# Weight-block sums of the seven-product duals: accumulating DMAs on GpSimd's queue in place of VectorE and GpSimd adds

## The chip, the cores and the metric

The kernel runs on one core of one Trainium2 chip. A core has TensorE (PE in the profile, with its weight loads as PEld), VectorE (DVE), ScalarE (ACT), GpSimd (POOL) and SyncE (SP), and 16 DMA engines that all queues share. The metric is the device time of one execution in microseconds, the median of several runs; lower is better.

## What is computed

One layer of a streaming encoder on a sequence of 1024 tokens with 1024 channels, all in fp32: a mixing sub-layer and a feed-forward sub-layer, each behind an RMS norm that is scaled and shifted by a condition vector.

```python
h = rms_norm(x, norm_mix_g) * (1.0 + sc1) + sh1
proj = h @ w_in                                   # 1024 -> 7 x 1024 columns
y_a = (b_s * causal_dwconv(c_s * v_s, conv_short_w)) @ w_short_out
u = causal_dwconv(v_c * sigmoid(gl_c), conv_conf_w) + conv_conf_b    # width 31
y_b = silu(layer_norm(u, conf_ln_g, conf_ln_b)) @ w_conf_out
x = x + g1 * ((g_a * y_a + g_b * y_b) @ w_o)
h2 = rms_norm(x, norm_ffn_g) * (1.0 + sc2) + sh2
a, bgate = split(h2 @ w_ffn_in)                   # 1024 -> 2 x 2816
x = x + g2 * ((silu(a) * bgate) @ w_ffn_out)
return rms_norm(x, final_norm_g)
```

## The kernel before

**Numbers as two parts.** Every fp32 operand of a matrix product is cut into a high and a low part that TensorE takes at its fast rate. For a weight block `raw` in SBUF, `split_w` (line 195) makes `wh`, a rounded copy written by ScalarE (line 201), and `wl = raw - wh`, written by VectorE or GpSimd (line 202). `mm3` (from line 269) then issues three matmuls per block: wh with the high and the low part of the activations (lines 273 and 274), and wl with the high part (line 276).

**Seven products for eight.** The input projection, the FFN input and all but the last part of the FFN output are done in duals: two by two blocks of the weights (11, 12, 21, 22) and of the activations, multiplied by a Winograd-like scheme with seven block products. The products come in the order `PRODUCTS = "1265734"` (line 91). Products 1, 2 and 4 use the weight blocks 11, 12 and 22 as loaded. The other four use sums of blocks:

- s1 = 21 + 22, for product 5 (line 222),
- 21 = 21 + 11, in place, for product 7 (line 223),
- 11 = 11 + s1, in place, for product 6 (line 224),
- 12 = 12 + 11, in place, after 11 has become the sum, for product 3 (line 226).

The first three are made when the weights of product 6 are prepared, the fourth when those of product 3 are. There are 12 duals in the input projection (`eng=nc.gpsimd`, so sums and `wl` are GpSimd's), 11 in the FFN input and 6 in the FFN output (both with VectorE). Blocks are 128x1024 fp32 (512 KB), in the FFN output 128x768 (384 KB). The first two duals of the FFN input are `early`: their blocks 21, 22 and 11 are loaded again when product 6 is prepared, s1 takes the place of 22, and 12 and 22 are loaded again for products 3 and 4. In all other duals the four blocks are loaded once, when product 1 is prepared, and s1 is written to a buffer of its own, `raw_tile(n)`.

**Buffers.** `raw_tile` (line 182) takes the buffers in turn from pools that hold five raw tiles together, and six from the second part of the FFN input on. `wh` and `wl` have three buffers each. `next_w` (line 241) prepares the weights of a product two products ahead. Weights are loaded by SP's queue (line 189).

**Other work on the queues.** In the input projection VectorE also computes the width-31 convolution (line 604), and SP stores and later loads the gated short-conv operands (`q_store`). In the FFN input the hidden values are combined, split on ScalarE and VectorE into three stage buffers, and stored to DRAM by DMAs on GpSimd's queue (`hid<-stage`, line 841). The FFN output reads them back by DMAs on GpSimd's queue (`th<-hid` and `tl<-hid`, line 867), six loads of 256 KB for each product, into a pool of 58 tiles. The order of the instructions on each engine's queue, DMA issues included, isn't the order of the code: a planner puts them in order by the times at which it computes them to be ready, with the order of the code as priority, and the chip then keeps to that order. A DMA that has to wait for a semaphore holds its issuing engine's queue.

Of the kernel before, what the change touches and what calls it, by code (L numbers as in the profile page):

```python
# [37 lines left out]
ALU = mybir.AluOpType  # L38
# [67 lines left out]
def block_kernel(ctx: ExitStack, tc: tile.TileContext, xT, c, vecs, ada, w_first, w_plain, w_duals,  # L106
                 w_short, w_conf, w_o, w_fi, w_fo, w_last, outT):
    nc = tc.nc
# [73 lines left out]
    def raw_tile(n=1024):  # L182

        raws.append(raws.pop(0))
        return raws[-1].tile([P, 1024], F32, tag="raw", name="raw")[:, :n]

    def load(src, n=1024):
        raw = raw_tile(n)
        nc.sync.dma_start(raw, src)
        return raw  # L190
# [4 lines left out]
    def split_w(raw, n, after=(), lo_engine=nc.vector):  # L195
        wh = whp.tile([P, 1024], F32R, tag="wh", name="wh")[:, :n]
        wl = wlp.tile([P, 1024], F32R, tag="wl", name="wl")[:, :n]
        with ExitStack() as order:
            for ins in after:
                order.enter_context(tc.issue_after(ins))  # L200
            nc.scalar.copy(wh, raw)  # L201
            lo_engine.tensor_tensor(wl, raw, f32(wh), ALU.subtract)  # L202
        return wh, wl

    def dual_units(mats, n, early=False, eng=nc.vector):

        a = {}

        def get(*blocks):
            for b in blocks:  # L210
                a[b] = load(mats[("11", "12", "21", "22").index(b)], n)

        def unit(m):
            if early:
                get(*{"1": ("11",), "2": ("12",), "6": ("21", "22", "11"), "3": ("12",), "4": ("22",)}.get(m, ()))
            elif m == "1":
                get("11", "12", "21", "22")
            if m in "12":
                return split_w(a["1" + m], n, (), eng)
            if m == "6":  # L220
                a["s1"] = a["22"] if early else raw_tile(n)
                eng.tensor_tensor(a["s1"], a["21"], a["22"], ALU.add)
                eng.tensor_tensor(a["21"], a["21"], a["11"], ALU.add)
                eng.tensor_tensor(a["11"], a["11"], a["s1"], ALU.add)
            elif m == "3":
                eng.tensor_tensor(a["12"], a["12"], a["11"], ALU.add)
            return split_w(a[{"6": "11", "5": "s1", "7": "21", "3": "12", "4": "22"}[m]], n, (), eng)

        return {m: (lambda m=m: unit(m)) for m in PRODUCTS}
# [695 lines left out]
    n = 2 * GROUP * P  # L925
# [164 lines left out]
```

## Time and profile before

| | us |
|---|---|
| median of 3 runs | 1544.36 (1543.83 to 1546.57) |
| profiled execution, own time | 1546.12 |
| its span, first to last instruction | 1544.4 |
| PE busy | 1472.5 |
| DVE busy | 1187.2 |
| ACT busy | 639.6 |
| POOL busy | 575.9 |

The profile is of one execution. Rows of the timeline read: start in us, duration in us, engine, line of the kernel, operation, output <- input by the program's names, shapes, count, and in brackets the idle time of the engine before it with what ended it. Rows of grouped instructions end in: busy us, mean ns of one | idle us before them, and what ended most of it. A DMA issue shows on its engine's queue for the issue alone; the rows of DMA issues give KB each and the median us from issue to landing. Matmuls are pipelined, so their rows overlap.

### The profile page before, as it was taken

The page shows a single profiled execution, that of the slowest core. Times are in us where ns is not written, and L with a number is a line of the kernel's source. Part 1 is how long each engine was busy: PE and PEld are TensorE (multiplying, and loading weights), DVE is VectorE, ACT ScalarE, POOL GpSimd, SP SyncE. Part 2 cuts the span into 40 slices and gives each one's busy share as a digit, 9 for nine tenths or more (in the row PEclk, how much of TensorE's full clock was granted, in tenths as well). Part 3 has the DMA queues.
Part 4 walks back from the last instruction along what each step waited for, and adds up shares of the span by engine and source line. Part 5 has one row for each costly group of instructions (what it writes and reads, how often), then busy time and mean ns, then how long its engine had stood idle before and what let it go on. Part 6 is the DMA issues. An engine that isn't in the chain of part 4 may idle for free.

```text
span 1544.4 us, 17865 instructions
## 1 busy us (share of the span) xinstructions
PE 1472.5 (95%) x6466; PEld 1208.6 (78%) x6466; DVE 1187.2 (77%) x1543; ACT 639.6 (41%) x896; POOL 575.9 (37%) x491
## 2 busy tenths in 40 slices
PE   5799999999999998989899989999999999999996
PEld 3588887888887887768788868888888888788885
DVE  7887899999998965656865798876767665677756
ACT  6563334333333342344334564444444443221235
POOL 1316778688768883310111101100100016445005
PEclk9999999999999999999999999999999999999998
DMA  9332214223222269455754428544444449999403
GB/s 369 143 100 75 95 55 164 68 96 109 96 82 95 92 230 386 144 184 164 243 191 166 164 82 258 191 150 150 151 150 156 156 151 348 349 308 274 125 14 110
DMA packets 88024, 256.16 MB, mean 166 GB/s; under 512 B 10112, under 2 KB 12288, under 8 KB 87936
## 3 DMA queue, kind: packets, MB, share of 16 engines
q1 hardware_dynamic: 47248, 147.01, 28.5%
q0 software_dynamic: 36944, 95.44, 19.1%
q10 hardware_dynamic: 3744, 12.58, 2.0%
q8 instruction: 50, 0.82, 0.2%
q14 instruction: 38, 0.31, 0.1%
HBM read 188.41 MB, written 66.58 MB: 165 GB/s over the span
## 4 chain that ended last, share of the span: by engine, by line
PE 47%; DVE 3%; issue 1%; ACT 0%; DVEq 0%; ACTq 0%
PE x L276 7%; PE x L273 7%; PE x L274 7%; PE z L273 4%; PE z L274 4%; PE z L276 4%; PE y L273 3%; PE y L276 2%; PE y L274 2%; PE mix L276 2%; PE mix L273 2%; PE mix L274 2%; PE yb L274 1%; PE yb L276 1%; PE yb L273 1%
## 5 line engine op out<-in xcount | busy, mean ns | idle before, releaser
L201 ACT CAST wh<-raw 128x1024 fp32r<-128x1024 f32 (+2 forms) x260 | 262.1, 1009 | 439.5 <-PE x L274 99.7
L202 POOL TENSOR_TENSOR wl<-raw,wh 128x1024 fp32r<-128x1024 f32 (+1 forms) x95 | 247.3, 2608 | 154.5 <-ACT wh L201 149.6
L202 DVE TENSOR_TENSOR wl<-raw,wh 128x1024 fp32r<-128x1024 f32 (+2 forms) x165 | 189.1, 1147 | 58.3 <-ACT wh L201 55.7
L604 DVE SCALAR_TENSOR_TENSOR c<-diff,vec,c 128x512 f32<-128x512 f32 x248 | 182.2, 749 | 3.9
L841 POOL DMA_DIRECT2D hid<-stage x71 | 37.8, 534 | 354.1 <-DVE stage L313 350.9
L273 PE MATMUL x<-th,wh 128*128 128x512 f32 x336 | 130.8, 389 | 0.0
L276 PE MATMUL x<-th,wl 128*128 128x512 f32 x336 | 130.7, 389 | 0.0
L274 PE MATMUL x<-tl,wh 128*128 128x512 f32 x336 | 130.7, 389 | 0.0
L604 DVE SCALAR_TENSOR_TENSOR c<-u,wsum,c 128x512 f32<-128x512 f32 x112 | 84.0, 750 | 2.0
L273 PE MATMUL x<-t2h,wh 128*128 128x512 f32 x184 | 73.8, 402 | 5.9 <-ACT wh L201 4.5
L276 PE MATMUL x<-t2h,wl 128*128 128x512 f32 x184 | 73.8, 402 | 4.7 <-POOL p L519 3.4
L274 PE MATMUL x<-t2l,wh 128*128 128x512 f32 x184 | 73.7, 401 | 0.1
L273 PEld LDWEIGHTS x<-th,wh 128*128 128x128 f32 x336 | 63.1, 188 | 13.2 <-issue 0.3
L274 PEld LDWEIGHTS x<-tl,wh 128*128 128x128 f32 x336 | 63.1, 188 | 13.2
L276 PEld LDWEIGHTS x<-th,wl 128*128 128x128 f32 x336 | 63.1, 188 | 13.1
L273 PE MATMUL z<-th,wh 128*128 128x512 f32 x168 | 65.4, 389 | 1.5 <-ACT wh L201 1.5
L258 DVE CUSTOM_DVE_ANT_0 raw<-raw,cs,vec 128x1024 f32<-128x1024 f32 x24 | 30.7, 1281 | 45.7 <-DMA raw<-in_ada 45.7
L276 PE MATMUL z<-th,wl 128*128 128x512 f32 x168 | 65.4, 389 | 0.0
L274 PE MATMUL z<-tl,wh 128*128 128x512 f32 x168 | 65.4, 389 | 0.0
L312 ACT CAST stage<-g 128x512 fp32r<-128x512 f32 x62 | 38.3, 620 | 56.5 <-DMA hid<-stage 29.3
L273 PE MATMUL yb<-zsh,wh 128*128 128x512 f32 x128 | 49.5, 400 | 10.4 <-ACT zsh L304 9.4
L313 DVE TENSOR_TENSOR stage<-g,stage 128x512 fp32r<-128x512 f32 x62 | 42.5, 688 | 20.0 <-ACT stage L312 20.0
(819 smaller groups left out, 4087.5 us busy)
## 6 DMA issues: line engine op xcount, KB each, us to landing
hid<-stage POOLq DMA_DIRECT2D x71, 512.0 KB, 4.3
raw<-in_w_fi SPq DMA_DIRECT2D x50, 512.0 KB, 4.3
raw<-in_w_duals SPq DMA_DIRECT2D x48, 512.0 KB, 3.5
th<-hid POOLq DMA_DIRECT2D x71, 256.0 KB, 6.1
tl<-hid POOLq DMA_DIRECT2D x71, 256.0 KB, 6.3
ada<-in_ada SPq DMA_DIRECT2D x24, 512.0 KB, 7.5
raw<-in_ada SPq DMA_DIRECT2D x24, 512.0 KB, 4.3
raw<-in_w_fo SPq DMA_DIRECT2D x24, 384.0 KB, 6.1
```

Source lines behind the costliest of these rows:

```text
L201: nc.scalar.copy(wh, raw)
L202: lo_engine.tensor_tensor(wl, raw, f32(wh), ALU.subtract)
L258: nc.vector.tensor_tensor_reduce(out=raw, in0=raw, in1=cs, scale=1.0, scalar=col(V_ADA, b), op0=ALU.mult, op1=ALU.add, accum_out=modc(b),)
L273: nc.tensor.matmul(ps, wh, xh, start=first, stop=False, skip_group_check=again)
L274: nc.tensor.matmul(ps, wh, xl, start=False, stop=False, skip_group_check=again)
L276: mm3.ins = nc.tensor.matmul(ps, wl, xh, start=False, stop=last, skip_group_check=again).ins
L312: nc.scalar.copy(hi, src)
L313: nc.vector.tensor_tensor(lo, src, f32(hi), ALU.subtract)
L604: nc.vector.scalar_tensor_tensor(out=out, in0=src[:, s : s + H], scalar=wt, in1=acc, op0=ALU.mult, op1=ALU.add)
L841: nc.gpsimd.dma_start(hid_dram[key], s)
```

## The change

The sums are no longer instructions of VectorE or GpSimd. Each is a DMA issued from GpSimd's queue that adds one SBUF tile to another (`accum_op=ALU.add`). Since an accumulating DMA adds to what its destination holds, s1 of a dual that isn't early is now made by loading block 22 a second time into the buffer of s1, and adding 21 to it.

```diff
             if m == "6":
-                a["s1"] = a["22"] if early else raw_tile(n)
-                eng.tensor_tensor(a["s1"], a["21"], a["22"], ALU.add)
-                eng.tensor_tensor(a["21"], a["21"], a["11"], ALU.add)
-                eng.tensor_tensor(a["11"], a["11"], a["s1"], ALU.add)
+                a["s1"] = a["22"] if early else load(mats[3], n)
+                nc.gpsimd.dma_start(a["s1"], a["21"], accum_op=ALU.add)
+                nc.gpsimd.dma_start(a["21"], a["11"], accum_op=ALU.add)
+                nc.gpsimd.dma_start(a["11"], a["s1"], accum_op=ALU.add)
             elif m == "3":
-                eng.tensor_tensor(a["12"], a["12"], a["11"], ALU.add)
+                nc.gpsimd.dma_start(a["12"], a["11"], accum_op=ALU.add)
             return split_w(a[{"6": "11", "5": "s1", "7": "21", "3": "12", "4": "22"}[m]], n, (), eng)
```

## The prediction

> **What bounds the kernel now.** I read the page first, then busy time by stage, then what TensorE (PE) waits for, and last the timeline of one dual of each stage. The first two lines are busy time by engine and the chain that ended last, by engine.
>
> ```profile
> PE 1472.5 (95%) x6466; PEld 1208.6 (78%) x6466; DVE 1187.2 (77%) x1543; ACT 639.6 (41%) x896; POOL 575.9 (37%) x491
> ...
> PE 47%; DVE 3%; issue 1%; ACT 0%; DVEq 0%; ACTq 0%
> ```
>
> Then busy us by stage: input projection in duals, FFN input, FFN output (columns PE, PEld, DVE, ACT, POOL, granted clock, DMA share, GB/s).
>
> ```profile
> 110.00:590.00 480.00, 475.12 (x2082) 392.24 (x2081) 421.18 (x523) 183.74 (x249) 361.91 (x164) 0.99 0.32 110
> 925.00:1315.00 390.00, 389.73 (x1709) 322.07 (x1708) 278.88 (x348) 171.92 (x249) 61.66 (x116) 0.99 0.57 186
> 1315.00:1490.00 175.00, 173.48 (x765) 143.11 (x764) 118.08 (x152) 39.87 (x51) 55.62 (x105) 1.00 0.74 231
> ```
>
> The sums exist in these three stages (and at 870 to 925, the head of the FFN), and PE is busy 99% of each: 475 of 480, 389.7 of 390, 173.5 of 175 us. VectorE and GpSimd are not the bound, so taking work off them pays only where PE waits for them. Those waits (total, times, longest):
>
> ```profile
> PE mu L632 <- DVE tot L629: 4.8, 1, 4.8
> PE x L273 <- ACT wh L201: 4.5, 1, 4.5
> ...
> PE x L276 <- POOL p L519: 3.4, 1, 3.4
> ```
>
> About 13 us is the most that can be won; the 4.5 us is the one that a sum causes directly.
>
> **What is removed.** Three sums in a row and a fourth per dual, 29 duals.
>
> ```profile
> L201 ACT CAST wh<-raw 128x1024 fp32r<-128x1024 f32 x202 | 212.0, 1051 | 319.1 <-PE z L274 61.7 <-issue 55.0 <-PE x L274 37.3
> ...
> L222 POOL TENSOR_TENSOR raw<-raw 128x1024 f32<-128x1024 f32 x12 | 29.5, 2456 | 41.5 <-DVE wl L202 39.4 <-DVE c L604 1.4
> ```
>
> In the 12 duals of the input projection four POOL adds of about 2.5 us, some 120 us of POOL; in 11 FFN-input duals four DVE adds of 1.22 us (the L222 row at 1104.17 below), 54 us; in six FFN-output duals four of 0.96 us (the row at 1386.06), 23 us. All of it lies beside PE, except at the head of the FFN.
>
> **What comes in.** 116 accumulating DMAs on POOL's queue, and 27 reloads of block 22 on SP's (12 + 9 + 6 duals that are not early). Within one dual they form a chain: s1 += 21 needs the reload landed; 21 += 11 overwrites what the first one reads, so POOL waits for its landing; 11 += s1 waits for the second. Only then can ScalarE cast 11 for product 6. Three adds that cost 3.7 us (DVE) or 7.5 us (POOL) become a reload and three complete DMA round trips. The price of an accumulating DMA from SBUF to SBUF is in no row. The nearest rows (KB, us to landing):
>
> ```profile
> hid<-stage POOLq DMA_DIRECT2D x71, 512.0 KB, 4.3
> raw<-in_w_fi SPq DMA_DIRECT2D x50, 512.0 KB, 4.3
> raw<-in_w_duals SPq DMA_DIRECT2D x48, 512.0 KB, 3.5
> th<-hid POOLq DMA_DIRECT2D x71, 256.0 KB, 6.1
> ...
> raw<-in_w_fo SPq DMA_DIRECT2D x24, 384.0 KB, 6.1
> ...
> x_dram<-x POOLq DMA_DIRECT2D x16, 256.0 KB, 3.0
> ```
>
> POOL's own stores go from 3.0 us for 256 KB to 4.3 for 512 KB: 1.3 us per 256 KB. Lower end for 512 KB: the second operand is read for nothing, 4.3 us. If it counts as 1 MB moved: 4.3 + 2.6 = 6.9. Upper end, two full transfers one after the other: 8.6. I take the middle of the first two, 5.6 us, as the nearest rows are those of POOL's stores, plus 0.4 us per link for POOL's issue and a weight op that stands in front: 6.0 us a link. For 384 KB the same steps give 3.65 and 5.6, middle 4.6, 5.0 with the 0.4.
>
> The Trainium skill, "Collectives: The Full Stack", The bandwidth ceiling, says that a reducing DMA is slowed by its second source read and not by the add; "DMA: Bandwidth & Descriptors", Anatomy of one DMA, puts a POOL-issued DMA at 2.0 us plus bytes at 436 GB/s. Together, as an estimate, 4.4 us for 1 MB read, 4.8 with the 0.4, by which the sum below would come out at no loss in two of three stages. The same fit would give 3.2 us for the hid store, which took 4.3 here, so the trace is above it.
>
> **Input projection.** One dual: the last weight split of the dual before, its first sum, and product 6's first matmul:
>
> ```profile
> 263.39 2.40 POOL L202 TENSOR_TENSOR wl<-raw,wh 128x1024 fp32r<-128x1024 f32 x1 [3.03 <-ACT wh L201]
> 265.86 2.40 POOL L222 TENSOR_TENSOR raw<-raw 128x1024 f32<-128x1024 f32 x1
> ...
> 289.44 0.39 PE L273 MATMUL x<-t2h,wh 128*128 128x512 f32 x1
> ```
>
> Five raw buffers serve five blocks, so s1 gets its buffer only when the previous dual's block 22 is split, at 265.79 (263.39 + 2.40); the sum starts 0.07 us later. After the change the reload starts there. To product 6 there are 289.44 - 265.79 = 23.65 us, less the cast 1.05 and the POOL split 2.4: 20.2. Less the reload 3.5: 16.7, or 5.6 us a link. A link of 6.0 is late by 3 x 0.4 = 1.2 us a dual; over 11 duals (the first has its data long before) 13 us. The DMA wait itself holds POOL, and behind it stand the splits wl of products 1 and 2, which PE needs 10 to 16 us before product 6: another 0.5 us a dual, 5 us. Behind the reload on SP stand the next blocks' loads and the q stores, which come later anyway: nothing. Term: **+18 us**.
>
> **FFN input.** The same with DVE splits; POOL's hid store is shown since it shares the queue:
>
> ```profile
> 1102.91 1.23 DVE L202 TENSOR_TENSOR wl<-raw,wh 128x1024 fp32r<-128x1024 f32 x1 [4.22 <-ACT wh L201]
> 1104.17 1.22 DVE L222 TENSOR_TENSOR raw<-raw 128x1024 f32<-128x1024 f32 x1
> ...
> 1119.09 0.53 POOL L841 DMA_DIRECT2D hid<-stage  x1 [24.41 <-DVE stage L313]
> ...
> 1129.06 0.39 PE L273 MATMUL x<-t2h,wh 128*128 128x512 f32 x1
> ```
>
> From 1104.14 to 1129.06 are 24.9; less cast 1.05 and split 1.23, 22.6; less the reload 4.3, 18.3: 6.1 us a link against 6.0. Term: **0**, and no reserve. POOL stands idle 24.4 us before the hid store, which covers the first two links; the third and the fourth accumulate fall among the stores. If they are ahead in the queue, the stage buffers (three) come free later and ScalarE waits with its casts; that is the cost if the cover goes.
>
> **FFN output.** Here a dual lasts 28 us, and POOL's queue carries the bursts of th and tl loads. The page's DMA line, then one dual in a gap between bursts:
>
> ```profile
> DMA  9332214223222269455754428544444449999403
> ```
>
> ```profile
> 1384.88 0.95 DVE L202 TENSOR_TENSOR wl<-raw,wh 128x768 fp32r<-128x768 f32 x1
> 1386.06 0.96 DVE L222 TENSOR_TENSOR raw<-raw 128x768 f32<-128x768 f32 x1 [0.24 <-DMA raw<-in_w_fo]
> ...
> 1404.41 0.39 PE L273 MATMUL x<-th,wh 128*128 128x512 f32 x1
> ```
>
> From 1385.83 to 1404.41 are 18.6; less the split 0.95 and a cast of 0.8 (three quarters of the 1.05 above, as 768 of 1024 columns), 16.8; less a reload of 6.1, 10.7: 3.6 us a link. A link of 5.0 is late by 3 x 1.4 = 4.2 us. In a burst (four to five slices at 9 in the DMA line) a POOL load of 256 KB lands after 6.1 where a quiet store takes 3.0, so I add 3.1 to each link: 3 x 4.5 = 13.5 us late. The th and tl tiles of a burst come free only as PE uses them up, so a stalled PE thins it; I count three duals of each sort: 3 x 4.2 + 3 x 13.5 = 53. Term: **+53 us**. Behind the waiting accumulates stand th and tl loads, for which PE waits a group later; with that much lead I cost them at nothing.
>
> **Head of the FFN.** Two early duals whose sums stand in DVE's line:
>
> ```profile
> 923.13 1.05 ACT L201 CAST wh<-raw 128x1024 fp32r<-128x1024 f32 x1 [5.28 <-DVE raw L224]
> ...
> 924.23 0.80 PE L273 MATMUL x<-t2h,wh 128*128 128x512 f32 x1 [4.54 <-ACT wh L201]
> ```
>
> Here DVE is late, not the data, and POOL is nearly free. The DMAs can run ahead while DVE makes the tokens' operands. Gain 4.5 us at most, and the splits next in DVE's line are then late; I take **-4**. The other waits in the list (mean of the conv, memset on POOL) may shrink too, -2.
>
> **Sum:** 18 + 0 + 53 - 4 - 2 = +65 us on the profiled span of 1544.4: 1609. The profiled execution took 1546.1 with what lies around its span; the runs without a profile have a median of 1544.36, so the span stands for them within 0.1 and **1609 us** is the prediction.
>
> **Rivals.**
> A, the chain is hidden and the time is the same or a little less. It decides at a link of 5.6 us in the projection, 6.1 in the FFN input and 3.6 to 4 in the FFN output. At the lower end (4.3 + 0.4 = 4.7, and 3.65 + 0.4 = 4.05 for 384 KB) the first two cost nothing, quiet output duals 1.4 each, burst ones perhaps 4: between -6 and +10 us, 1538 to 1554. For it: the 3.5 us loads and a DMA share of 0.32 and 0.57. Against: the hid row of 4.3 for one plain pass. The two pages of the Trainium skill named above lead here too. Chance 0.24: faster 0.12, same 0.07, slower 0.05.
> B, the accumulate runs at half rate or worse. At 7.5 us (7.9 a link): projection 3 x 2.3 x 11 = 76, FFN input 3 x 1.8 x 9 = 49, FFN output about 85: +210, 1750. At 8.6, 1830. For it: two reads per write, and th's 6.1 for 256 KB. Against: half the 16 engines' time is free. Chance 0.24.
> C, the planner that orders each engine's queue puts product 5, whose s1 is ready after one link, ahead of 6. That gives PE 5 us of other work and takes most of the projection's loss and part of the output's: +15 to +35, 1560 to 1580. For it: POOL's order already departs from the written one (first sum of a dual ahead of its first split). Against: it orders by planned times, and a DMA planned shorter than it is changes nothing. Chance 0.10.
>
> **Chances.** Forecast (1575 to 1680) 0.42, A 0.24, B 0.24, C 0.10. Within 0.2%, about what a measurement of this kernel can tell from no change (1541.3 to 1547.5): faster 0.12, same 0.08, slower 0.80. The forecast's own range is 1575 to 1680. The range given reaches into A, which leaves out the best of it, and into B as far as 1750: 1538 to 1750.
>
> **What would show it.** The median time to landing of the new raw<-raw rows decides: 5.6 forecast, under 4.7 rival A, over 7 rival B. In the waits of PE, x <- ACT wh at L201 should appear once per dual, short in the projection, long in the FFN output, with L201 in turn waiting for a DMA. If the matmul order at the start of a dual is 1, 2, 5, 6, it is C. The forecast is wrong if the FFN output is not the stage that loses most, or if hid stores on POOL wait for raw<-raw and pull the FFN input down.

## The result, and the profile after

The changed kernel takes 1666.69 us (median of 4 runs, 1660.23 to 1676.03), the kernel before 1544.09 us in the same session (4 runs): ratio 1.0796, 95% interval 1.0742 to 1.0849. That is 123 us slower; the forecast was 1609, 65 us slower. The profiled execution has a span of 1662.9 us.

From the page of the kernel after: busy time by engine, the clock of PE and the DMA share in 40 slices, and the chain that ended last, by engine and by line.

```profile
PE 1500.9 (90%) x6466; PEld 1215.4 (73%) x6466; DVE 1129.4 (68%) x1475; ACT 633.0 (38%) x896; POOL 542.5 (33%) x559
...
PEclk9999999999999999989999999999999996899898
DMA  9345556465555696556656697777777799979712
...
PE 9%; DMA 3%; issue 1%; DVE 1%; ACT 0%; POOL 0%; DVEq 0%; ACTq 0%; POOLq 0%
DMA raw<-raw 2%; PE x L273 1%; PE x L276 1%; PE x L274 1%; PE y L276 1%; PE y L274 1%; PE y L273 1%; PE z L274 1%; PE z L273 1%; PE z L276 1%; DMA th<-hid 0%; ACT wh L201 0%; DMA raw<-in_w_fo 0%; DVE sq L982 0%; DVE y L995 0%
```

The diff did what it says: DVE is busy 58 us less and POOL 33 us less. But PE, which does exactly the same 6466 matmuls, is busy 28 us longer (1472.5 before) and idle 90 us longer. The chain before was 47% PE. Now it is 9% PE and 3% DMA: the profile can follow only a small part of it, but the largest single line of that part is `DMA raw<-raw`, which didn't exist before.

Busy us by stage of the kernel after (PE, PEld, DVE, ACT, POOL, granted clock, DMA share, GB/s): input projection, FFN input, FFN output.

```profile
124.70:617.20 492.50, 470.66 (x2017) 382.30 (x2015) 415.82 (x515) 174.98 (x239) 260.06 (x159) 0.98 0.61 168
902.50:1357.40 454.90, 431.40 (x1852) 348.24 (x1851) 270.49 (x356) 196.97 (x290) 92.28 (x145) 0.99 0.79 222
1357.40:1600.60 243.20, 184.52 (x757) 147.54 (x756) 102.45 (x136) 37.82 (x51) 85.20 (x145) 0.87 0.84 232
```

The edges are the first matmuls of the stages. The kernel before, cut at the same matmuls:

```profile
124.90:590.40 465.50, 460.62 (x2017) 380.24 (x2016) 410.14 (x518) 178.37 (x241) 349.50 (x160) 0.99 0.33 113
877.10:1308.60 431.50, 425.13 (x1852) 348.42 (x1851) 319.59 (x403) 199.54 (x290) 58.29 (x110) 0.99 0.53 173
1308.60:1482.00 173.40, 171.88 (x758) 141.79 (x757) 120.47 (x156) 39.94 (x51) 59.54 (x113) 1.00 0.79 247
```

All three stages lost: 27.0, 23.4 and 69.8 us. Length less PE busy is PE's idle time. It grew by 17.0 us (4.9 to 21.8), 17.1 us (6.4 to 23.5) and 57.2 us (1.5 to 58.7). The rest of each loss is matmuls that took longer: 10.0, 6.3 and 12.6 us.

**The link.** Landing of the new transfers and of two neighbours (KB, us from issue to landing):

```profile
raw<-raw POOLq DMA_DIRECT2D x92, 512.0 KB, 4.6
hid<-stage POOLq DMA_DIRECT2D x71, 512.0 KB, 5.6
...
raw<-in_w_fi SPq DMA_DIRECT2D x59, 512.0 KB, 5.3
...
raw<-raw POOLq DMA_DIRECT2D x24, 384.0 KB, 4.5
```

An accumulating DMA takes 4.6 us, where the prediction took 5.6. The neighbours slowed down by 1.0 to 1.3 us (4.3 before).

**Who waits.** PE's waits (total, times, longest):

```profile
PE x L273 <- ACT wh L201: 47.4, 6, 26.8
PE x L273 <- ACT g L816: 16.7, 12, 4.0
...
PE z L273 <- ACT wh L201: 9.2, 1, 9.2
...
PE x L273 <- ACT sig L535: 4.4, 2, 4.1
PE x L276 <- POOL wl L202: 4.2, 5, 1.6
PE x L273 <- ACT p L535: 3.3, 2, 2.5
```

Two kinds. `wh L201` is the weight itself that is late. `g L816`, `sig` and `p L535` are ScalarE's copies of finished products out of PE's accumulators: PE waits there though the weights it needs next may be ready. One projection dual on three engines shows how that comes about:

```profile
319.91 0.88 POOL L222 DMA_DIRECT2D raw<-raw  x1 [4.08 <-issue]
...
324.74 0.88 POOL L223 DMA_DIRECT2D raw<-raw  x1 [1.51 <-DMA raw<-raw]
...
330.92 0.88 POOL L224 DMA_DIRECT2D raw<-raw  x1 [2.70 <-DMA raw<-raw]
...
335.53 1.04 ACT L201 CAST wh<-raw 128x1024 fp32r<-128x1024 f32 x1 [10.53 <-DMA raw<-raw]
336.48 0.58 ACT L535 COPY m<-x 128x512 f32<-128x512 f32 x1
...
337.11 0.50 PE L273 MATMUL x<-t2h,wh 128*128 128x512 f32 x1 [2.64 <-ACT m L535]
```

The links are 4.83, 6.18 and 4.61 us apart. ScalarE stands 10.53 us at the cast of product 6, which waits for the third link. The copy behind it in its queue starts only then, and PE waits 2.64 us for that copy.

**FFN output.** The first dual, then the clock before it, after it and, in the projection, right behind PE's wait of 2.95 us that ended at 225.75:

```profile
1343.39 0.33 SPq L189 DMA_DIRECT2D raw<-in_w_fo  x1
...
1367.72 0.89 POOL L222 DMA_DIRECT2D raw<-raw  x1 [0.95 <-DMA tl<-hid]
...
1376.08 0.88 POOL L223 DMA_DIRECT2D raw<-raw  x1 [1.76 <-issue]
...
1381.45 0.89 POOL L224 DMA_DIRECT2D raw<-raw  x1 [1.30 <-DMA raw<-raw]
...
1391.62 2.30 ACT L201 CAST wh<-raw 128x768 fp32r<-128x768 f32 x3 [19.63 <-DMA raw<-raw]
...
1392.50 0.79 PE L273 MATMUL x<-th,wh 128*128 128x512 f32 x1 [26.78 <-ACT wh L201]
```

```profile
1355.00:1365.50 10.50, 10.50 (x48) 8.54 (x46) 4.78 (x7) 2.84 (x5) 8.10 (x16) 1.00 1.20 353
...
1392.00:1396.50 4.50, 4.00 (x9) 2.95 (x10) 2.70 (x3) 1.92 (x3) 3.47 (x7) 0.50 1.27 398
...
226.20:229.50 3.30, 3.30 (x10) 2.53 (x9) 3.19 (x6) 3.30 (x6) 2.78 (x2) 0.50 0.00 0
```

Block 22 was asked for again at 1343.39, but the first sum is issued 24.3 us later: POOL's queue in between holds th and tl loads and hid stores. Then the three links take 23.9 us. After the 26.78 us stall the granted clock is 0.50, so the stall goes on costing.

### The profile page after: what moved, and what is told of

Read it like the earlier page. It is cut to its first block, busy times and chain, and to the rows that moved or that the text cites. A ratio compares the mean times of both kernels' runs of the same rounds, so it can differ in the third digit from the quotient of the medians.

```text
span 1662.9 us, 18058 instructions
## 1 busy us (share of the span) xinstructions
PE 1500.9 (90%) x6466; PEld 1215.4 (73%) x6466; DVE 1129.4 (68%) x1475; ACT 633.0 (38%) x896; POOL 542.5 (33%) x559
## 5 line engine op out<-in xcount | busy, mean ns | idle before, releaser
L201 ACT CAST wh<-raw 128x1024 fp32r<-128x1024 f32 (+2 forms) x260 | 260.1, 1008 | 551.9 <-DMA raw<-raw 244.7
L202 POOL TENSOR_TENSOR wl<-raw,wh 128x1024 fp32r<-128x1024 f32 (+1 forms) x95 | 243.8, 2611 | 144.4 <-ACT wh L201 141.0
L202 DVE TENSOR_TENSOR wl<-raw,wh 128x1024 fp32r<-128x1024 f32 (+2 forms) x165 | 188.6, 1148 | 124.6 <-ACT wh L201 121.9
L273 PE MATMUL x<-th,wh 128*128 128x512 f32 x336 | 136.1, 405 | 52.9 <-ACT wh L201 47.0
L276 PE MATMUL x<-th,wl 128*128 128x512 f32 x336 | 135.2, 402 | 0.5 <-POOL wl L202 0.5
L274 PE MATMUL x<-tl,wh 128*128 128x512 f32 x336 | 134.5, 400 | 0.0
L273 PEld LDWEIGHTS x<-th,wh 128*128 128x128 f32 x336 | 65.6, 195 | 70.4 <-ACT wh L201 49.1
L273 PE MATMUL x<-t2h,wh 128*128 128x512 f32 x184 | 77.9, 425 | 25.6 <-ACT g L816 15.1
L222 POOL DMA_DIRECT2D raw<-raw x29 | 25.7, 885 | 229.4 <-DMA raw<-in_w_fi 46.5
L276 PE MATMUL x<-t2h,wl 128*128 128x512 f32 x184 | 76.7, 417 | 5.4 <-POOL wl L202 3.3
L841 POOL DMA_DIRECT2D hid<-stage x71 | 41.3, 591 | 117.7 <-DVE stage L313 116.3
L276 PEld LDWEIGHTS x<-th,wl 128*128 128x128 f32 x336 | 65.2, 194 | 16.8 <-DVE wl L202 2.2
L273 PE MATMUL z<-th,wh 128*128 128x512 f32 x168 | 66.4, 395 | 9.3 <-ACT wh L201 9.2
L273 PEld LDWEIGHTS x<-t2h,wh 128*128 128x128 f32 x184 | 37.1, 202 | 40.1 <-ACT g L816 19.6
L276 PE MATMUL z<-th,wl 128*128 128x512 f32 x168 | 66.1, 393 | 0.3 <-DVE wl L202 0.3
```

The source lines that it names most:

```text
L222: nc.gpsimd.dma_start(a["s1"], a["21"], accum_op=ALU.add)
L273: nc.tensor.matmul(ps, wh, xh, start=first, stop=False, skip_group_check=again)
L274: nc.tensor.matmul(ps, wh, xl, start=False, stop=False, skip_group_check=again)
L276: mm3.ins = nc.tensor.matmul(ps, wl, xh, start=False, stop=last, skip_group_check=again).ins
L841: nc.gpsimd.dma_start(hid_dram[key], s)
```

## The experiments

Theory 1, formed from the profile after: the price isn't the transfers but that **each sum waits for the landing of the one before and every queue is in order**. ScalarE stands at product 6's cast with PE's evacuations behind it, and POOL's sums stand among other DMAs. Rival: the transfers themselves (71 MB more are moved, 327.2 for 256.2) slow everything down. A narrower rival for the FFN input: the hid stores behind the waiting sums on POOL.

Lengths of the stages in the profiled execution of each kernel, in us; before's profile has a span of 1544.4:

| kernel | projection | middle | FFN input | FFN output | tail | median | ratio to before, 95% |
|---|---|---|---|---|---|---|---|
| before | 465.5 | 286.7 | 431.5 | 173.4 | 62.5 | 1544.09 | |
| after | 492.5 | 285.3 | 454.9 | 243.2 | 62.3 | 1666.69 | 1.0742 to 1.0849 |
| traffic | 489.0 | 286.2 | 430.3 | 197.2 | 62.4 | 1593.93 | 1.0308 to 1.0362 |
| order_125 | 473.8 | 285.0 | 451.5 | 244.1 | 62.3 | 1646.82 | 1.0641 to 1.0688 |
| cast6_pool | 471.1 | 284.7 | 453.5 | 248.8 | 62.2 | 1648.23 | 1.0648 to 1.0718 |
| bufs | 472.9 | 280.6 | 437.3 | 233.0 | 62.3 | 1613.00 | 1.0404 to 1.0494 |
| bufs_125 | 468.7 | 276.8 | 436.6 | 236.9 | 62.2 | 1605.65 | 1.0372 to 1.0418 |
| hid_on_sp | 491.6 | 286.9 | 458.3 | 246.8 | 62.3 | 1670.45 | 1.0764 to 1.0878 |
| hid_sp_cast6 | 471.4 | 282.6 | 448.4 | 246.9 | 62.4 | 1641.89 | 1.0569 to 1.0703 |
| t_on_sp | 490.8 | 280.9 | 460.8 | 246.0 | 62.7 | 1670.21 | 1.0783 to 1.0862 |
| half_t | 491.7 | 284.1 | 459.0 | 206.0 | 62.1 | 1629.09 | 1.0504 to 1.0602 |
| no_chain | 461.9 | 288.3 | 442.7 | 208.1 | 62.3 | 1590.18 | 1.0294 to 1.0324 |
| m3_only | 458.7 | 284.9 | 430.7 | 189.0 | 62.8 | 1553.00 | 1.0053 to 1.0081 |
| e4_early | 465.5 | 286.1 | 432.8 | 171.4 | 62.2 | 1547.29 | 1.0015 to 1.0049 |

The FFN input again, cut at the first matmuls of its duals: us over the kernel before, whose two early duals take 88.7 us, the third dual 38.1 and the other eight 304.6.

| kernel | two early duals | third dual | other eight |
|---|---|---|---|
| after | 2.3 | 7.0 | 14.0 |
| traffic | -1.2 | 0.0 | 0.0 |
| order_125 | 16.5 | 0.0 | 3.5 |
| cast6_pool | 8.1 | 3.7 | 10.2 |
| bufs | -5.5 | 8.2 | 3.2 |
| bufs_125 | 0.7 | 1.7 | 2.8 |
| hid_on_sp | -0.1 | 11.7 | 15.3 |
| hid_sp_cast6 | 4.5 | 12.4 | 0.0 |
| t_on_sp | 2.7 | 10.0 | 16.6 |
| half_t | 5.1 | 8.8 | 13.7 |
| no_chain | 6.1 | 5.1 | 0.0 |
| m3_only | -1.5 | 0.7 | 0.0 |
| e4_early | 1.3 | 0.0 | 0.0 |

The edits of t_on_sp and half_t are meant for the next stage, and yet their three columns differ from after's by up to 3 us. Differences of that size aren't read here.

### Traffic without a chain (traffic)

The kernel before, with two plain stores of block 22 on POOL's queue at each of products 6, 5, 7 and 3. Nothing reads what they store.

```diff
+    spare = []
...
+            if m in "6573" and not early:
+                for _ in range(2):
+                    nc.gpsimd.dma_start(dram.tile([P, n], F32, name=f"spare{len(spare)}"), a["22"])
+                    spare.append(0)
             return split_w(a[{"6": "11", "5": "s1", "7": "21", "3": "12", "4": "22"}[m]], n, (), eng)
```

> The kernel before, its sums on VectorE and GpSimd as they were, plus eight plain 512 KB (384 KB) stores of block 22 to unused DRAM per dual that is not early, two each when the weights of products 6, 5, 7 and 3 are prepared: 216 stores that nothing waits for, on GpSimd's queue. They move at least as many bytes through the 16 DMA engines as the change does, without its chain of waits. Chain theory (the loss is the time from the freed buffer over reload and three round trips to product 6, passed on by the in-order queues of ScalarE and GpSimd): 1544 to 1560 us. Traffic theory (DMA share went from 0.33 to 0.61 in the projection and from 0.54 to 0.79 in the FFN input, hid stores from 4.3 to 5.6 us): 1600 us or more, with all three stages longer.

Neither number came: 1593.93. By stage it reads better. First the stages, then who waits, and one stall of the FFN output, in this kernel (its L202, L203, L223, L278 and L281 are L201, L202, L222, L273 and L276 of the others):

```profile
126.00:615.00 489.00, 468.97 (x2018) 381.48 (x2017) 424.26 (x518) 178.48 (x242) 399.35 (x250) 0.99 0.56 205
901.10:1331.40 430.30, 423.89 (x1851) 347.47 (x1850) 318.17 (x403) 197.95 (x290) 93.24 (x177) 0.99 0.75 258
1331.40:1528.60 197.20, 174.20 (x757) 142.81 (x756) 119.96 (x156) 39.34 (x51) 89.07 (x166) 0.95 0.96 320
```

```profile
POOL spare L230 <- DMA raw<-in_w_duals: 80.9, 11, 38.5
...
PE x L281 <- POOL wl L203: 15.6, 10, 3.7
```

```profile
1387.94 0.96 DVE L223 TENSOR_TENSOR raw<-raw 128x768 f32<-128x768 f32 x1 [13.91 <-DMA spare<-raw]
...
1391.88 0.80 PE L278 MATMUL x<-th,wh 128*128 128x512 f32 x1 [18.64 <-ACT wh L202]
```

In the FFN input the DMA share is 0.75, near after's 0.79, with more bytes per second (258 against 222 GB/s), and the stage is as long as before: plain traffic is not what costs there. The other two stages aren't to be used. In the projection POOL still makes all sums and splits, so the added stores held the splits up (80.9 us of waiting at the head of POOL's queue). The FFN output is 24 us longer at a share of 0.96, but 18.64 us of that are one stall: VectorE's first sum waited 13.91 us for added stores, which stood behind a row of th and tl loads on POOL and still read the buffer that the sum writes. So what traffic alone costs in the FFN output isn't shown by this kernel.

### Product 5 ahead of product 6 (order_125)

s1, for product 5, is ready after one link; product 6 needs three.

```diff
-PRODUCTS = "1265734"
+PRODUCTS = "1256734"
...
-            if m == "6":
+            if m == "5":
                 a["s1"] = a["22"] if early else load(mats[3], n)
```

> The changed kernel with product 5 ahead of product 6 (order 1, 2, 5, 6, 7, 3, 4), the sums made when the weights of 5 are prepared. Product 5 needs one link of the chain and gives PE 5.4 us of work (4.1 in the FFN output) while the other two run. Chain theory: of +25 us in the projection and +23 in the FFN input at most 5 to 8 each are left, of +70 in the FFN output some 20 go; 1595 to 1620 us. If the loss is traffic, or GpSimd's queue being held, the order of products changes little: 1655 to 1675.

1646.82 lies between the two ranges. The projection recovers 18.7 of its 27.0 us. The FFN input recovers 3.4 and the FFN output nothing, which theory 1 in this form didn't expect. By dual the FFN input reads otherwise: from the third dual on, 3.5 us are left of after's 21.0, as theory 1 expected, and the two early duals are 16.5 us longer than before. There VectorE waits 10.3 and 3.0 us for the weights that the condition vector meets (`ada<-in_ada`), for which it doesn't wait in the kernel before; how much of the 16.5 us that is isn't shown. ScalarE's waits over the whole stage, first after's, then this kernel's:

```profile
ACT wh L201 <- DMA raw<-raw: 61.1, 10, 8.8
ACT stage L312 <- DMA hid<-stage: 55.2, 34, 3.4
```

```profile
ACT stage L312 <- DMA hid<-stage: 95.2, 21, 10.2
```

The wait for the sums is gone from ScalarE and a wait for the hid stores has grown by 40 us in its place; 86.1 of the 95.2 us fall in the nine later duals, where they cost PE almost nothing.

### Product 6's cast on GpSimd (cast6_pool)

The same chain, but ScalarE doesn't stand at its end.

```diff
-            nc.scalar.copy(wh, raw)
+            cast(wh, raw)
...
-            return split_w(a[{"6": "11", "5": "s1", "7": "21", "3": "12", "4": "22"}[m]], n, (), eng)
+            return split_w(a[{"6": "11", "5": "s1", "7": "21", "3": "12", "4": "22"}[m]], n, (), eng, nc.gpsimd.tensor_copy if m == "6" else nc.scalar.copy)
```

> The changed kernel with the cast of product 6's weights (the one that waits for the third link) on GpSimd in place of ScalarE, so that ScalarE's queue holds no wait for the chain of three. If PE stalls in the projection and the FFN input because ScalarE stands at this cast and evacuates finished products late: PE's waits for ACT at L535 and L816 go (some 30 us), 1630 to 1645 us, projection and FFN input 10 to 20 us shorter each. If PE stalls because the weights of product 6 themselves are late: no gain, as the cast on GpSimd is slower by 1 to 2 us, 1665 to 1685.

1648.23 lies between the two ranges as well. The projection recovers 21.4 us, with the order of the products, the chain and all transfers unchanged. So what PE lost there came through ScalarE's queue, not through product 6's weights. In the FFN input, where 10 to 20 us were expected, it is nearly nothing (1.4): ScalarE's wait for hid stores is now 111.2 us.

### One raw buffer more (bufs), and with the other order (bufs_125)

The raw pool gets a tile and the t pool, which holds th and tl, gives one up.

```diff
-    tp = pool("t", 58)
-    rawp = pool("raw", 3)
+    tp = pool("t", 57)
+    rawp = pool("raw", 4)
...
-    raws = [rawp] * 3 + [rawbp] * 2
+    raws = [rawp] * 4 + [rawbp] * 2
```

> The changed kernel with one raw buffer more (six for five blocks in the projection, seven for five later) and 57 instead of 58 tiles for the hidden values. The reload of block 22 then finds a free buffer before the previous dual's last split, so the chain starts some 4 to 5 us earlier in each dual. If the chain's length from freed buffer to product 6 sets the loss: projection from 492.5 us to 470 to 478 and FFN input from 455 to 440 to 448, 1630 to 1645 in all. If it doesn't start with the buffer (traffic, or GpSimd's queue alone): within 5 us of the changed kernel in both stages.

> Both of the levers that shortened the projection, one raw buffer more (t pool 57 for 58) and product 5 ahead of product 6. Theory 1, only the lateness of the chain at its first user counts: projection at most 468 us, FFN input at most 436, so both back at before's 465.5 and 431.5 within 4 us; FFN output 225 to 235, since the links among the th and tl loads stay slow; whole kernel 1590 to 1608. Rival, there is a part that neither buffers nor order take away: projection 472 or more, and no faster than the extra buffer alone (1613).

With one buffer more, the reload needn't wait for the last split of the dual before, so the chain starts earlier. That recovers 19.6 us of the projection, 17.6 of 23.4 in the FFN input and 10 in the FFN output. Both levers together come within 3.2 and 5.1 us of before in the first two stages, and 1605.65 us is just below the extra buffer alone (1613.00; the intervals of the ratios overlap). The projection missed its bound of 468 and the FFN input its 436 by under 1 us; the FFN output, expected at 225 to 235, stayed at 236.9. The middle stage, whose weights come through the same raw buffers, is 5 to 9 us shorter than after's, and the two early duals of bufs are 5.5 us shorter than before's. So part of the gain may have nothing to do with the sums; a buffer more for the kernel before wasn't tried.

### Hid stores on SP's queue (hid_on_sp), and with the cast on GpSimd (hid_sp_cast6)

```diff
-        nc.gpsimd.dma_start(hid_dram[key], s)
+        nc.sync.dma_start(f32(hid_dram[key]), f32(s))
```

> The changed kernel with the stores of the hidden values (71, 512 KB) issued by SP instead of GpSimd, where they stand behind the accumulating DMAs' waits. If the FFN input loses its 23 us because these stores are issued late, the three stage buffers come free late and ScalarE stands at its stage cast: ScalarE's wait for hid<-stage falls from 50 us to about 20 and the FFN input from 455 to 435 to 442 us. If it loses them by ScalarE's cast of product 6 waiting for the third link: 450 to 458, unchanged.

> Both: hidden stores on SP and the cast of product 6 on GpSimd. If the two queues (GpSimd's with the stores, ScalarE's with the cast) each alone keep the FFN input late, as moving the cast alone left it at 453.5 us, then both together bring it to 431 to 438 us, and the projection stays at the 471 us that the cast alone gave: 1615 to 1630 in all. If the FFN input stays over 448, neither queue is what holds it.

Taking the hid stores off POOL's queue gave nothing: FFN input 458.3. ScalarE's wait for hid stores fell only to 48.7 us, and that for the sums rose to 84.9. As the only cause the narrow rival falls. With the cast moved as well, the stage takes 448.4, which is over the 448 that was to mean that neither queue holds it. By dual the answer is the opposite. The last eight duals of hid_sp_cast6:

```profile
1022.99:1327.63 304.64, 304.64 (x1346) 252.25 (x1344) 174.04 (x218) 126.79 (x182) 51.03 (x70) 1.00 0.79 233
```

PE is never idle there, with the chain and all its transfers in place. Moving the stores alone leaves 15.3 us of loss in these duals, moving the cast alone 10.2, and both together none: what one edit frees, the other queue takes, and the two queues together are what costs. The 16.9 us that this kernel still loses all lie in the first three duals; in the third VectorE waits 6.8 us for `ada<-in_ada`, and what else costs there stays open.

### The th and tl loads on SP's queue (t_on_sp), and half of them (half_t)

```diff
-            nc.gpsimd.dma_start(t, hid_dram[key][:, s])
+            nc.sync.dma_start(f32(t), f32(hid_dram[key][:, s]))
```

> The changed kernel with the th and tl loads of the hidden values (142 loads, 256 KB) issued by SP in place of GpSimd, so that GpSimd's queue in the FFN output carries the accumulating DMAs nearly alone. If the 26.8 us and 11.6 us stalls of PE in the FFN output come from accumulates that stand behind th and tl loads on GpSimd's queue: FFN output from 239 to 185 to 200 us, 1615 to 1630 us in all. If the chain's own length does it: FFN output stays at 225 to 245 and the time within 1650 to 1675.

half_t loads only the high parts and uses them in place of the low ones too:

```diff
-        hl = t_pair("t")
-        for t, s in zip(hl, halves):
-            nc.gpsimd.dma_start(t, hid_dram[key][:, s])
-        return hl
+        t = hl_tile("th")
+        nc.gpsimd.dma_start(t, hid_dram[key][:, halves[0]])
+        return t, t
```

> The changed kernel with only the high parts of the hidden values loaded in the FFN output (71 loads instead of 142) and used in the place of the low parts too, so part of the product is left out. If the links of the chain are slow there (7 to 10 us instead of 4.5) because the bursts of th and tl loads fill the DMA engines and GpSimd's queue: FFN output from 243 to 190 to 205 us. If the chain's length alone, at 4.5 us a link against 3.6 to 4 that fit, does it: 225 us or more.

t_on_sp, first dual of the FFN output, and busy time and DMA share from its first sum to its third:

```profile
1372.24 0.89 POOL L222 DMA_DIRECT2D raw<-raw  x1 [11.79 <-DMA raw<-in_w_fo]
1380.00 0.88 POOL L223 DMA_DIRECT2D raw<-raw  x1 [6.33 <-DMA raw<-raw]
1388.08 0.88 POOL L224 DMA_DIRECT2D raw<-raw  x1 [4.02 <-DMA raw<-raw]
```

```profile
1372.20:1388.10 15.90, 0.00 (x0) 0.00 (x0) 0.00 (x0) 0.00 (x0) 5.50 (x10) 0.50 1.07 356
```

Moving the loads to the other queue moved the wait: POOL no longer issues th and tl loads, but now the reload of block 22 stands behind them on SP, and L222 waits for it. The links are about 8 us apart here, and both waits in between end with a landing: the first two sums take 7.2 and 7.5 us to land, at a DMA share of 1.07, where the median in the kernel after is 4.5. So in this burst it isn't the wait for a turn on POOL's queue that makes a link slow. POOL still issues a hid store and six loads `x<-x_dram` between them, so that the full DMA engines do it is likely, but not shown apart from these. The stage stays at 246.0. Loading half as much takes 37 of its 69.8 lost us away (206.0, 1 us above the range). The two together: about half of the FFN output's loss is the sums' meeting with this burst, and moving the burst to another queue doesn't help. half_t takes fewer of the t tiles, too, so it doesn't part the transfers from the room for them.

### As many accumulates, without the chain (no_chain)

In the 27 duals that aren't early the three sums take blocks that none of them writes, so none waits for another. What is computed is then not the layer.

```diff
+                b = ("21", "11", "s1") if early else ("22", "12", "12")
-                nc.gpsimd.dma_start(a["s1"], a["21"], accum_op=ALU.add)
-                nc.gpsimd.dma_start(a["21"], a["11"], accum_op=ALU.add)
-                nc.gpsimd.dma_start(a["11"], a["s1"], accum_op=ALU.add)
+                nc.gpsimd.dma_start(a["s1"], a[b[0]], accum_op=ALU.add)
+                nc.gpsimd.dma_start(a["21"], a[b[1]], accum_op=ALU.add)
+                nc.gpsimd.dma_start(a["11"], a[b[2]], accum_op=ALU.add)
```

> As many accumulating DMAs, bytes and reloads as after, but in the 27 duals that are not early the three sums of product 6 use other sources (s1 += 22, 21 += 12, 11 += 12), so that none waits for another's landing; only the reload and one landing stay between the free buffer and the cast. The output is therefore not the reference's. Theory 1, the three landings in a row are the loss: projection back to 465 to 470 us (after 492.5, before 465.5), FFN input at most 436 (after 454.9, before 431.5), FFN output 200 to 220 (after 243.2, before 173.4), whole kernel 1565 to 1595. Rival, the number and bytes of the accumulates and the reload are the loss: every stage within 5 us of after, 1650 or more.

1590.18: theory 1's range. Its stages, and the last eight duals of the FFN input:

```profile
124.80:586.70 461.90, 458.12 (x2017) 378.12 (x2016) 407.01 (x514) 176.50 (x239) 264.11 (x159) 1.00 0.63 175
875.00:1317.70 442.70, 429.32 (x1852) 350.28 (x1851) 270.34 (x356) 199.40 (x290) 97.57 (x155) 0.98 0.83 233
1317.70:1525.80 208.10, 180.81 (x757) 146.06 (x756) 102.15 (x136) 38.47 (x52) 79.98 (x135) 0.93 0.93 259
...
1013.10:1317.74 304.64, 304.64 (x1346) 252.25 (x1344) 172.20 (x218) 132.45 (x190) 74.47 (x122) 1.00 0.85 239
```

The projection moves as much as after does (share 0.63 against 0.61) and is 3.6 us shorter than before: there the chain is the whole net loss. The FFN output gets back half, as with half_t. The FFN input gets back 12.2 of 23.4 us, where at most 436 us was expected. But the edit leaves the chain in the two early duals. The last row is the other eight duals: PE is never idle in them, at a DMA share of 0.85, so there the chain is all of the loss, and neither the transfers nor slower hid stores cost anything. The 11.2 us that are left lie in the two early duals (6.1) and the third (5.1).

### The fourth sum alone (m3_only)

```diff
-                a["s1"] = a["22"] if early else load(mats[3], n)
-                nc.gpsimd.dma_start(a["s1"], a["21"], accum_op=ALU.add)
-                nc.gpsimd.dma_start(a["21"], a["11"], accum_op=ALU.add)
-                nc.gpsimd.dma_start(a["11"], a["s1"], accum_op=ALU.add)
+                a["s1"] = a["22"] if early else raw_tile(n)
+                eng.tensor_tensor(a["s1"], a["21"], a["22"], ALU.add)
+                eng.tensor_tensor(a["21"], a["21"], a["11"], ALU.add)
+                eng.tensor_tensor(a["11"], a["11"], a["s1"], ALU.add)
```

> Only the fourth sum (12 += 11, for product 3) is a DMA, in all 29 duals; the first three are VectorE's and GpSimd's as before. It stands alone: one landing of about 4.6 us, with product 3 not due for three more products. Theory 1, the landings in a row are the loss: 1540 to 1552, no stage over 4 us longer than before. Rival, each accumulate costs by itself (a fourth of the 122 us): about 1575.

1553.00, 0.67% over before and 1 us above theory 1's range. The first two stages lose nothing: the projection is even 6.8 us shorter, as POOL is busy less there (322 us for 349) and PE's waits for POOL, 4.9 us before, are gone. The FFN output is 15.6 us longer, against the expected 4 at most, and nearly all of it is one wait:

```profile
1327.32 0.53 POOL L867 DMA_DIRECT2D tl<-hid  x1
1327.88 0.88 POOL L226 DMA_DIRECT2D raw<-raw  x1
...
1334.03 2.30 ACT L201 CAST wh<-raw 128x768 fp32r<-128x768 f32 x3 [25.33 <-DMA raw<-raw]
...
1334.91 0.80 PE L273 MATMUL z<-th,wh 128*128 128x512 f32 x1 [14.62 <-ACT wh L201]
```

The sum takes about 6 us to land. ScalarE stood 25.33 us, because the sum's issue is the last of a long row of th and tl loads on POOL, many of which wait in turn. Even a single sum off every chain can stall PE if its queue is long.

### The two early duals alone (e4_early)

```diff
-    in_units = [dual_units([w_fi[d, m] for m in range(4)], 1024, d < 2) for d in range(N_IN)]
+    in_units = [dual_units([w_fi[d, m] for m in range(4)], 1024, d < 2, dma=d < 2) for d in range(N_IN)]
```

(Not shown: a flag in `dual_units` that chooses between the DMA and the engine's add.)

> Sums by DMA only in the two early duals at the head of the FFN, where the prediction saw a gain of 4 us, as VectorE is late there and not the data. By the prediction: 1539 to 1542. By the theory that a row of landings on the way to a cast costs more than a late VectorE: 1543 to 1550.

1547.29, 0.32% over before (0.15 to 0.49), so the gain of 4 us isn't there. PE's 4.5 us wait at the head, the one a sum caused directly, is gone, and three others stand in its place: 1.39 us for an operand (`t2l`), 1.07 for a weight of the chain, 2.06 for ScalarE's copies, 4.5 again in all. ScalarE stood 6.53 us for a raw<-raw at 933.

## Why the prediction was right in direction and half in size

- **The bound.** Right: PE was the bound, and freeing VectorE (58 us) and GpSimd (33 us) bought nothing.
- **The link, 5.6 + 0.4 = 6.0 us.** Too dear. The landing is 4.6. From issue to issue, the medians over eleven of the twelve projection duals (the first makes its sums ahead of the stage) are 4.84 (first to second), 5.11 (second to third) and 4.65 (third to cast), 14.6 together. The Trainium skill ("Collectives: The Full Stack", The bandwidth ceiling, with "DMA: Bandwidth & Descriptors", Anatomy of one DMA) gave an estimate of 4.4 for this landing: near the 4.6 measured. By the sign that the prediction named, under 4.7, it is rival A, and rival A's time was 1538 to 1554. The price was A's and the time wasn't, so the failed step is the next one.
- **Projection, +18; measured +27.0.** "To product 6 there are 23.65 us" counted one user of the chain, product 6's first matmul. The chains of these eleven duals took 14.5 to 16.7 us and so fit the 16.7 us computed. PE stalled in five duals all the same: 12.2 us for ScalarE's copies in four of them, 4.5 us for splits on POOL. Four of these five are among the five in which a link took over 6 us. In two of the four (2.6 and 4.1 us) the copy stands right behind the waiting cast; in the other two (3.0 and 2.5) ScalarE last waited for VectorE or PE, and the trace doesn't lead back to a sum. That the loss came through ScalarE is shown by cast6_pool, which gets 21.4 us back by moving one cast. The right question was when ScalarE reaches the cast, and what is queued behind it. The idle time grew by 17 us, close to the 18 by accident of two errors; the other 10 are slower matmuls, a term the sum lacked.
- **FFN input, 0; measured +23.4.** The same step. The prediction named the cost if the cover goes (ScalarE waiting for stage buffers) and gave it no price. By the sign that it set itself, hid stores held by raw<-raw, it was wrong here. The fuller picture: ScalarE waits 61.1 us for sums and 55.2 for hid stores (25.9 before), and taking away either alone gives nothing or little. In the last eight duals, 14.0 of the 23.4 us, the cause is shown: without the chain (no_chain), or with the chain but both waits off their queues (hid_sp_cast6), the loss is 0.0. The other 9.4 us fall on the two early duals and the third. With one buffer more 2.7 of them are left, and the chain in the two early duals alone costs 1.3 (e4_early), which is within the scatter; what makes up the rest stays open.
- **FFN output, +53; measured +69.8.** It is the stage that lost most, as forecast, by other terms. "Each link in a burst is 3.1 us longer", in three duals, was wrong: in five of the six duals the links are 4.0 to 6.2 us apart, and only the first dual has 8.36, 5.37 and 10.17. "Behind the waiting accumulates stand th and tl loads" had it the wrong way round for the largest stalls: the accumulates stand behind the loads. Idle time: 26.8 us for that first dual, 11.6 for product 6 of the fifth and 9.2 for a fourth sum, both issued behind a row of loads on POOL, and 8.6 for product 6 of three others (12.6 for three quiet duals was forecast). To this come 12.6 us of longer matmuls, at a clock of 0.87 for 1.00.
- **Head of the FFN, -4.** Wrong; e4_early shows no gain.
- **Rivals.** B falls (4.6 us, not 7.5). C didn't happen by itself: product 6 still came third; made by hand (order_125), it took 20 us off, less than the 30 to 50 that C's range supposed.

On the span the sum is short by 53 us (118 measured, 65 forecast): 9 in the projection, 23 in the FFN input, 17 in the FFN output, and 4 for gains that didn't come. 28 us of the 118 are longer matmuls, which no term of it held.

## What to carry to other kernels

Price a chain of DMAs not at its last user alone but at every queue on which one of its links or its consumer waits: what stands behind the waiting instruction is late by the same time, and what stands ahead of a link in its queue is added to it. If sums must be DMAs, start the chain early with one buffer more, let a product with a short chain go first, and keep the consumer's wait off the engine that empties PE's accumulators. A sum that is off every chain can be moved at no cost in a stage whose queue is short (projection and FFN input of m3_only); by the table, the fourth sum by DMA in the projection alone would give an estimate of 1544.4 - 6.8 = about 1538 us. That kernel wasn't run, and 17 executions of the kernel before lie between 1539.27 and 1546.75, so a gain of this size would need several runs to show.

## What the runs showed of the hardware

- A POOL issue of an accumulating DMA is busy 0.88 us, that of a plain load or store 0.53 us.
- 384 KB and 512 KB accumulate in nearly the same time by their medians, 4.5 and 4.6 us. But the blocks of 384 KB stand in the stage with the bursts; three of them in a quiet moment, at 1487 to 1497, took 3.9 to 4.1 us.
- Stalls cost twice. After 26.78 us without work the granted clock was 0.50 for the next 4.5 us. The Trainium skill ("TensorE: Matmul & The Clock Gate", HAM oscillation — how this bites in real kernels) has the rule that PE's idle gaps shouldn't exceed about 3.4 us; the trace agrees for this gap. But shorter gaps were followed by it too: a single one of 2.95 us, ended at 225.75, by a clock of 0.50 over 226.2 to 229.5, and one of 2.14 us, ended at 1586.65, by 0.50 over 1588.1 to 1591.4. One of 2.51 us, ended at 1131.46, was followed by 1.00. So gaps of 2 to 3 us can already lower the clock, and which of them do isn't told by their length alone.
